# Second feed-forward of a two-layer diffusion backbone: more block steps between down tiles, x parked in DRAM, first queries ahead of later values

## The chip, the core and the metric

The kernel runs on one core of a Trainium2 chip. Its engines are PE (TensorE, matrix products; PEld is its weight load), DVE (VectorE), ACT (ScalarE) and POOL (GpSimd); SP (SyncE) issues nearly all DMAs. The metric is the device time of one execution in microseconds, the median of several runs. Everything is float32; each product of two float32 matrices is made from rounded high parts and remainders, as three matmuls.

## The reference

Two layers work on 512 tokens of width 1024 (`x`), with 256 context tokens.

```python
for i in range(DEPTH):                      # 2 layers
    h = modulate(rms_norm(x, norm_g[i, 0]), sh1, sc1)        # sh, sc, g: silu(c) @ mod_w[i] + mod_b[i]
    if i % 2 == 0:   # 4 global heads (qk-norm, rotary) and 4 windowed heads with a sink
        y, yc = attention_mixers(h, hc, ...)
    else:            # real part of a 2-D FFT over 4 channel groups, then a linear map
        y = fourier_mix(h) @ w_f
    x = x + g1 * rms_norm(y, norm_g[i, 1])
    h = modulate(rms_norm(x, norm_g[i, 2]), sh2, sc2)
    x = x + g2 * rms_norm(conv_ffn(h, ...), norm_g[i, 3])

def conv_ffn(h, w_up, conv_w, conv_b, w_down):
    u = h @ w_up                            # 1024 -> 2 x 2816
    u = depthwise width-3 convolution of u along the tokens, plus conv_b
    gate, val = jnp.split(u, 2, axis=-1)
    return (jax.nn.silu(gate) * val) @ w_down
```

## The kernel before

Data lie with channels on the 128 partitions: `xT`, `yT`, `hh` and `hl` are 128 x 8 x 512. The code is written as one long program; a scheduler then places each instruction on its engine's queue by its place in the text and by when its inputs and buffers are expected, and adds the semaphores. So the order in a queue can differ from the written one. `held`, `fence` and `follow` pin some of it.

**Splits.** `split(h, l, src)` (its two instructions have line L121) makes the high part on ACT and the remainder on DVE; `mm3` (L98, L99, L100) issues the three matmuls. Weights come by `raw` (L130, three buffers, loaded on SP's queue) and are split into `wpair` (five buffers for each part).

**The feed-forward** (`ffn`, run for layers 0 and 1). 2816 hidden channels are 22 blocks of 128, `fi` 0 to 21. An *up step* makes gate and value of one block. A plain step is 2 x 8 x 3 matmuls 512 columns wide. A *block step* (`seven_products`, for the `fi` in `SEVEN[l]`) splits the product in 2 x 2 blocks and needs seven block products instead of eight, 7 x 4 x 3 matmuls 256 wide; DVE adds weights for it (L1124 to L1127), ACT copies partial sums (L1158 to L1168) and DVE merges them (L1166, L1169). Its combined inputs are made once by `seven_inputs`, at `fi == SUMS[l]`, in place in `yT`. After either, `conv` (L1220 on ACT, L1221 and L1223 on DVE) and `gated` (L1233, L1234 and a split) leave the pair `gs[fi]` in `xp.pair` (four buffers of two blocks).

**Down tiles.** `GROUPS` cuts the 22 blocks in three groups of 8, 6 and 8. After the last up step of a group, eight tiles `d` of 128 output channels are made in a row: `weights(d)` loads and splits the down weights, `part(d, hs)` runs the matmuls (24 or 18 of 512 columns) and copies to `yT` (first group) or adds to it (L1341). The remaining `gemv` of layer 1 (L422, L425 on DVE; products of the conditioning vector) is pumped along with the tiles. The last group runs on halves of the tokens: first half of all tiles, then `mid` (norm sums, `boundary`, `x_update` at L297 and L299 and the output DMAs of the first half) while PE makes the second half, then the second half's tail.

In layer 0, `gemv_jobs` already stores `xT` to the DRAM tile `away`, uses its memory for weights, and loads it back (L407, L434).

**Attention's projections.** After the global keys and values come three groups of `w_in` columns, in the order `kb` (windowed keys, three blocks of tokens), `vb` (windowed values, three blocks) and `qa` (queries of heads 0 and 1, two blocks; `q_out` norms and rotates them into `Q`, which is `yT`'s memory). `keys(0)` (transposes of `K` on PE) and `values(0)` are placed beside the query blocks. Beside all of them `gate`, a `gemv_early`, makes two modulation vectors on DVE (L476, L478): each takes eight 0.5 MB loads into five places, three in `yT` and two in the context's buffer. Then `queries_t(0)` transposes the first head's queries (L949) and attention begins, with the other queries' projections as filler.

Of the kernel before, what the change touches and what calls it, by code (L numbers as in the profile page):

```python
# [10 lines left out]
F32 = mybir.dt.float32  # L11
# [18 lines left out]

GROUPS = [(0, 8), (8, 6), (14, 8)]

# [3 lines left out]

SEVEN = [(5, 6, 8, 10, 12, 14, 15, 17, 18, 20), (8, 9, 11, 12, 14, 15, 17, 18, 20)]
NSKEW = [6, 5]
# [37 lines left out]
def kernel(ctx: ExitStack, tc: tile.TileContext, a):  # L76
# [380 lines left out]
    def gemv_early(jobs, places, accs, pps):  # L457
        ws = {}

        def load(n):  # L460
            if n < KC * len(jobs):
                (l, v), k = jobs[n // KC], n % KC
                ws[n] = places[n % len(places)]()
                SY.dma_start(out=ws[n], in_=a["mod_r"][6 * l + v - 2, k // 2][:, k % 2, :])

        for n in range(3):
            load(n)
        yield
        for n in range(3, len(places)):
            load(n)  # L470
        yield
        ends = []
        for n in range(KC * len(jobs)):
            acc, k = accs[n // KC], n % KC
            if k == 0:
                V.tensor_scalar(out=acc, in0=ws[n], scalar1=scol[:, 0, k:k + 1], scalar2=None, op0=ALU.mult)  # L476
            else:
                V.scalar_tensor_tensor(out=acc, in0=ws[n], scalar=scol[:, 0, k:k + 1], in1=acc, op0=ALU.mult,  # L478
                                       op1=ALU.add)
            load(n + len(places))  # L480
            yield
            if k == KC - 1:
                ends.append(gemv_end(*jobs[n // KC], acc, pps))
            elif k in (1, 3):
                for e in ends:
                    next(e, None)
        yield
        for _ in range(2):
            next(ends[-1], None)
            yield  # L490
# [37 lines left out]
    with ExitStack() as es:  # L528
# [29 lines left out]
        with ExitStack() as e1:  # L558
# [281 lines left out]
            blocks = [(hh, hl, 0, 2), (hh, hl, 2, 4), (ch, cl, 0, 0)]  # L840
            for g, kind in enumerate(["kb", "vb", "qa"]):
                ws = group_weights(g)
                if g == 2:
                    v_kv = []
                if g == 2:
# [351 lines left out]

    def ffn(l, xp, ready, pre, mid, gem, plain=None):
        ys = YStat(late=xp.pool if l == 0 else None)
        skew = NSKEW[l]  # L1200
# [31 lines left out]
        def gated(fi, cg, cv, f0):  # L1232
            S.activation(out=cg, in_=cg, func=AF.Silu)  # L1233
            V.tensor_tensor(out=cv, in0=cg, in1=cv, op=ALU.mult)  # L1234
# [4 lines left out]
            gs[fi] = (gh, gl)  # L1239


# [23 lines left out]
        else:  # L1265
# [30 lines left out]
            sweep(range(skew), halves[1], range(SWEEP[1], KC))  # L1296
            remod(1, *n2, R[1], eng=V)
            first[skew] = first[skew][:3] + (mk(pps, [P, T], F32, "mm", 6),)
        if l == 0:
            pump(gem)  # L1300
        cg = None
        for u, (fi, i, w, ps) in enumerate(first):
# [13 lines left out]
            :, :, NF:], scalar1=-1.0, scalar2=None, op0=ALU.mult)  # L1316
        for gi, (f0, nch) in enumerate(GROUPS):
            end = gi == len(GROUPS) - 1
            for fi in range(max(f0, FIRST), f0 + nch):
# [11 lines left out]
                if l == 0 and fi not in SEVEN[l]:  # L1331
                    pump(gem, GP[0])
            g_ = [gs[fi] for fi in range(f0, f0 + nch)]
            ws = {}

            def part(d, hs, ps=None):
                ps, sl = y_mm(pps, ws[d], g_, hs, True, ps)
                if gi == 0:
                    S.copy(out=yT[:, d, sl], in_=ps[:, sl])
                else:  # L1340
                    V.tensor_tensor(out=yT[:, d, sl], in0=yT[:, d, sl], in1=ps[:, sl], op=ALU.add)  # L1341
                if end:
                    ys.add(pps, yT[:, d, sl], hs)

            def weights(d):
                r = raw([P, nch, P], a["w_down%d" % gi][l, d])
                wh, wl = (xp.spare if end and 4 <= d < 7 else wpair)([P, nch, P])
                split(wh, wl, r)
                ws[d] = [(wh[:, c, :], wl[:, c, :]) for c in range(nch)]

# [265 lines left out]
def _layout(i):  # L1616
# [29 lines left out]
    out = {}  # L1646
    for h, (f0, n) in enumerate(GROUPS):
        out["w_down%d" % h] = wd[:, f0:f0 + n].transpose(0, 3, 2, 1, 4)
    wf = i["fourier_w_out"][0].reshape(4, 256, D)
# [25 lines left out]
```

## Time and profile before

| what | us |
|---|---|
| median of 3 runs | 1147.99 (1147.73 to 1148.07) |
| the profiled execution | 1147.63, of which the span is 1145.9 |
| PE busy / DVE busy / ACT busy / POOL busy | 1115.4 / 872.4 / 577.6 / 176.6 |
| second feed-forward from its first full-width up step to the last matmul of its last group | 801.6 to 1132.6 |
| its last group of down tiles | 1085.9 to 1132.6 |
| windowed keys, values and first queries to the start of attention | 73.2 to 127 |

The profile is one execution. "Busy" is the time in which an engine worked on instructions; waits and DMA issues are not counted. Matmuls are pipelined and their shown ends overlap the next one, so the distance between starts tells how long one takes. In rows of the timeline the columns are start, length, engine, line, operation, tiles (out<-in), shape and count, and in brackets the idle time before it with what ended it. In rows by line, the numbers behind the first bar are busy us and mean ns of one, behind the second the engine's idle time before them. In rows by window, busy us and counts of PE, PEld, DVE, ACT and POOL follow the length, then the granted PE clock, the DMA share and GB/s. DMA rows give KB each and us from issue to landing.

### The profile page before, as it was taken

To read this page: it belongs to the slowest core of one execution; us is meant where nothing else is said; L and a number is where in the kernel's file an instruction comes from. 1 tells how busy PE (TensorE), PEld (TensorE's weight loads), DVE (VectorE), ACT (ScalarE), POOL (GpSimd) and SP (SyncE) were. 2 spreads that over 40 slices of the span, in tenths; PEclk is the share of its full clock that TensorE was granted. 3 is DMA by queue.
4 is the path that set the end of the run, shared out by engine and by line. 5 is a ranking of instruction groups with operands and counts; after the bars stand their busy time and mean duration, and the time that the engine had idled before them with its cause. 6 is when DMAs were issued, how large, how long until landed. Compare 5 with 4: busy or idle time off the path is not lost.

```text
span 1145.9 us, 19121 instructions
## 1 busy us (share of the span) xinstructions
PE 1115.4 (97%) x7658; PEld 962.8 (84%) x7658; DVE 872.4 (76%) x1418; ACT 577.6 (50%) x1030; POOL 176.6 (15%) x184
## 2 busy tenths in 40 slices
PE   8999999999999999999999999899999999999995
PEld 5689988868898978887898898879887888899895
DVE  4678777765679976987998668878997498679745
ACT  4342356666665633552465445557743355256442
POOL 1136332521420000000000143610000000000023
PEclk9999999999999999999999999999999999999998
DMA  9676101075142355535525301920227123223212
GB/s 366 248 239 215 43 1 38 8 263 208 38 184 111 117 194 207 218 122 209 187 108 183 122 2 37 291 88 28 74 95 270 58 92 111 101 84 111 93 56 74
DMA packets 31745, 151.61 MB, mean 132 GB/s; under 512 B 3236, under 2 KB 7972, under 8 KB 19752
## 3 DMA queue, kind: packets, MB, share of 16 engines
q1 hardware_dynamic: 30504, 146.19, 35.9%
q0 software_dynamic: 1152, 4.19, 1.5%
q8 instruction: 60, 0.98, 0.4%
q14 instruction: 29, 0.24, 0.1%
HBM read 146.18 MB, written 4.19 MB: 131 GB/s over the span
## 4 chain that ended last, share of the span: by engine, by line
PE 84%; DVE 7%; ACT 5%; DMA 2%; issue 1%; POOL 0%; DVEq 0%; SPq 0%; ACTq 0%; POOLq 0%
PE mm L98 24%; PE mm L99 23%; PE mm L100 23%; PE PT L920 1%; ACT wh L121 1%; PE O L98 1%; PE gm L498 1%; PE gm L98 1%; PE O L99 1%; PE gm L100 1%; PE gm L99 1%; PE mm L173 1%; PE O L100 1%; DVE md_t L230 1%; DMA xT<-in_mod_r 1%
## 5 line engine op out<-in xcount | busy, mean ns | idle before, releaser
L121 ACT CAST wh<-raw 128x1024 fp32r<-128x1024 f32 (+2 forms) x189 | 180.4, 966 | 188.8 <-PE mm L99 131.3
L121 DVE TENSOR_TENSOR wl<-raw,wh 128x1024 fp32r<-128x1024 f32 (+3 forms) x179 | 203.4, 1144 | 62.8 <-ACT wh L121 62.5
L98 PE MATMUL mm<-hh,wh 128*128 128x256 f32 (+2 forms) x652 | 220.8, 339 | 1.4 <-ACT yT L895 1.0
L99 PE MATMUL mm<-hl,wh 128*128 128x256 f32 (+2 forms) x652 | 218.4, 335 | 0.0
L100 PE MATMUL mm<-hh,wl 128*128 128x256 f32 (+2 forms) x652 | 218.1, 335 | 0.0
L272 POOL TENSOR_TENSOR gacc<-gacc,sq 128x256 f32<-128x256 f32 (+1 forms) x33 | 28.4, 862 | 714.2 <-ACT sq L270 713.5
L98 PEld LDWEIGHTS mm<-hh,wh 128*128 128x128 f32 x652 | 122.5, 188 | 18.9 <-ACT sq L1160 2.8
L99 PEld LDWEIGHTS mm<-hl,wh 128*128 128x128 f32 x652 | 122.6, 188 | 14.0
L100 PEld LDWEIGHTS mm<-hh,wl 128*128 128x128 f32 x652 | 122.6, 188 | 13.8
L98 PE MATMUL mm<-xh,wh 128*128 128x512 f32 (+1 forms) x368 | 132.0, 359 | 0.0
L99 PE MATMUL mm<-xl,wh 128*128 128x512 f32 (+1 forms) x368 | 130.8, 356 | 0.0
L100 PE MATMUL mm<-xh,wl 128*128 128x512 f32 (+1 forms) x368 | 130.3, 355 | 0.0
L98 PE MATMUL mm<-zh,wh 128*128 128x256 f32 x304 | 86.8, 286 | 0.0
L99 PE MATMUL mm<-zl,wh 128*128 128x256 f32 x304 | 84.6, 278 | 0.0
L100 PE MATMUL mm<-zh,wl 128*128 128x256 f32 x304 | 84.3, 277 | 0.0
L98 PEld LDWEIGHTS mm<-xh,wh 128*128 128x128 f32 x368 | 69.3, 188 | 12.8 <-issue 2.1
L99 PEld LDWEIGHTS mm<-xl,wh 128*128 128x128 f32 x368 | 69.2, 188 | 11.1 <-issue 0.4
L100 PEld LDWEIGHTS mm<-xh,wl 128*128 128x128 f32 x368 | 69.2, 188 | 10.8
L1220 ACT ACTIVATE cv<-mm,cols 128x512 f32<-128x512 f32 x64 | 49.6, 776 | 26.5 <-PE mm L100 23.5
L98 PEld LDWEIGHTS mm<-zh,wh 128*128 128x128 f32 x304 | 57.2, 188 | 3.5 <-ACT sq L1163 2.7
L100 PEld LDWEIGHTS mm<-zh,wl 128*128 128x128 f32 x304 | 57.2, 188 | 0.0
L99 PEld LDWEIGHTS mm<-zl,wh 128*128 128x128 f32 x304 | 57.1, 188 | 0.0
(423 smaller groups left out, 2669.3 us busy)
## 6 DMA issues: line engine op xcount, KB each, us to landing
raw<-in_w_up SPq DMA_DIRECT2D x42, 1024.0 KB, 4.9
xT<-in_mod_r SPq DMA_DIRECT2D x20, 1024.0 KB, 4.9
raw<-in_w_down SPq DMA_DIRECT2D x32, 512.0 KB, 4.2
raw<-in_mod_p SPq DMA_DIRECT2D x8, 1024.0 KB, 5.0
raw<-in_w_in SPq DMA_DIRECT2D x6, 1024.0 KB, 7.9
raw<-in_w_down SPq DMA_DIRECT2D x16, 384.0 KB, 3.1
yT<-in_mod_r SPq DMA_DIRECT2D x10, 512.0 KB, 5.9
raw<-in_w_out SPq DMA_DIRECT2D x4, 1024.0 KB, 4.9
```

Of the source, the lines that this page charges most:

```text
L98: i = PE.matmul(out, lhsT=ah, rhs=bh, start=start, stop=False, skip_group_check=skip)
L99: PE.matmul(out, lhsT=ah, rhs=bl, start=False, stop=False, skip_group_check=skip)
L100: return i, PE.matmul(out, lhsT=al, rhs=bh, start=False, stop=stop, skip_group_check=skip)
L121: i = S.copy(out=h, in_=src), eng.tensor_tensor(out=l, in0=src, in1=f(h), op=ALU.subtract)
L173: PE.matmul(ps[:32, :src.shape[1]], lhsT=ones32, rhs=src, start=True, stop=True)
L230: V.scalar_tensor_tensor(out=t, in0=src, scalar=am, in1=R, op0=ALU.mult, op1=ALU.mult)
L272: G.tensor_tensor(out=self.acc[:, sl], in0=self.acc[:, sl], in1=sq[:, sl], op=ALU.add)
L498: PE.matmul(ps[32 * q:32 * q + 32, :], lhsT=spad[:, k, :], rhs=w[:, q * T:(q + 1) * T], start=k == 0, stop=k == KC - 1)
L920: PE.transpose(out=pt[:, j * P:(j + 1) * P], in_=Ps[j][:, off:off + P], identity=ident)
L1220: S.activation(out=cv, in_=ps, func=AF.Identity, bias=bc, scale=wc[1])
```

## The change

1. Layer 1's groups become 4, 6, 6 and 6 blocks, and block steps are made for all `fi` from 8 to 21 (14 instead of 9).
2. The down tiles of a group that isn't the last are no longer made in a row at its end: `down_tiles` is a generator that the next group's steps pump, as many tiles after step `fi` as `DOWN[fi]` says. `gemv` rides on the tiles of the second and third group.
3. With groups overlapping, more pairs are alive. After the modulation in layer 1 `xT` is stored to `away`, and its memory holds the pairs of `fi` 0 to 3 and later of 10 to 13; before the last group's tiles `xT` is loaded back.
4. In attention's projections the order becomes `kb`, `qa`, `vb`; `keys(0)` and `values(0)` follow the first value block; `gemv_early` loads its second vector into the two context places alone, since the queries now take `yT` earlier.
5. The down weights are laid out as one array for each layer and group.

```diff
-GROUPS = [(0, 8), (8, 6), (14, 8)]
+GROUPS = [[(0, 8), (8, 6), (14, 8)], [(0, 4), (4, 6), (10, 6), (16, 6)]]
...
-SEVEN = [(5, 6, 8, 10, 12, 14, 15, 17, 18, 20), (8, 9, 11, 12, 14, 15, 17, 18, 20)]
+SEVEN = [(5, 6, 8, 10, 12, 14, 15, 17, 18, 20), (8, 9, 10, 11, 12, 13, 14, 15, 16, 17, 18, 19, 20, 21)]
+
+DOWN = {8: 4, 9: 4, 10: 1, 11: 1, 12: 1, 13: 2, 14: 1, 15: 2, 16: 1, 17: 1, 18: 1, 19: 2, 20: 1, 21: 2}
...
         def load(n):
             if n < KC * len(jobs):
                 (l, v), k = jobs[n // KC], n % KC
-                ws[n] = places[n % len(places)]()
+                ws[n] = places[n % len(places) if n < KC else 3 + n % 2]()
...
-            load(n + len(places))
+            if n + len(places) < KC:
+                load(n + len(places))
+            for m in {3: (8,), 4: (9,)}.get(n, (n + 2,) if n >= KC else ()):
+                load(m)
...
-            for g, kind in enumerate(["kb", "vb", "qa"]):
+            for g, kind in ((0, "kb"), (2, "qa"), (1, "vb")):
...
-                        pump(gate, 2 if kind == "vb" else 1)
+                        pump(gate, 2 if kind == "qa" else 1)
...
-                        if t0 == 0:
-                            keys(0, [(mk(pps, [P, T], F32, "misc", 2), n) for n in (2, 4)])
-                        else:
-                            v_kv.append(values(0))
                         q_out(0, t0, ps)
+                    if kind == "vb" and kb == 2:
+                        keys(0, [(mk(pps, [P, T], F32, "misc", 2), n) for n in (2, 4)])
+                        v_kv.append(values(0))
...
-                gs["t"] = xp.pair([P, 2, T])
+                gs["t"] = places.pop(0) if l and (f0 == 0 or f0 == 10 and fi < 14) else xp.pair([P, 2, T])
...
+        def down_part(gi, w, g_, d, hs, ps=None, end=False):      # the former part(d, hs)
+        def down_weights(gi, nch, d, pairs):                      # the former weights(d)
+        def down_tiles(gi, nch, g_):
+            yield
+            for d in range(KC):
+                down_part(gi, down_weights(gi, nch, d, wpair), g_, d, [0, 1])
+                if gi:
+                    pump(gem, GP[1])
+                yield
...
             remod(1, *n2, R[1], eng=V)
+            SY.dma_start(out=away, in_=xT)
+            xp2 = mk(cp, [P, 2, 2, 2, T], F32R, "xT")
+            places = [(xp2[:, i, 0], xp2[:, i, 1]) for i in (0, 1, 0, 1)]
...
-        for gi, (f0, nch) in enumerate(GROUPS):
+        down = iter(())
+        for gi, (f0, nch) in enumerate(GROUPS[l]):
...
+                if l:
+                    pump(down, DOWN.get(fi, 0))
+            pump(down, 100)
+            if l and end:
+                xT = mk(cp, [P, KC, T], F32, "xT")
+                SY.dma_start(out=xT, in_=away)
             g_ = [gs[fi] for fi in range(f0, f0 + nch)]
+            if l and not end:
+                down = down_tiles(gi, nch, g_)
+                pump(down)
+                continue
```

More of the change, by code (lines that the diff above doesn't have):

```diff
@@ L844 @@
                     v_kv = []
-                if g == 2:
+                if g == 1:
                     w_q = group_weights(3)
@@ L1198, in ffn @@
     def ffn(l, xp, ready, pre, mid, gem, plain=None):
+        nonlocal xT
         ys = YStat(late=xp.pool if l == 0 else None)
@@ L1239, in gated @@
             gs[fi] = (gh, gl)
+        def down_part(gi, w, g_, d, hs, ps=None, end=False):
+            ps, sl = y_mm(pps, w, g_, hs, True, ps)
+            if gi == 0:
+                S.copy(out=yT[:, d, sl], in_=ps[:, sl])
+            else:
+                V.tensor_tensor(out=yT[:, d, sl], in0=yT[:, d, sl], in1=ps[:, sl], op=ALU.add)
+            if end:
+                ys.add(pps, yT[:, d, sl], hs)
+        def down_weights(gi, nch, d, pairs):
+            r = raw([P, nch, P], a["w_down%d%d" % (l, gi)][d])
+            wh, wl = pairs([P, nch, P])
+            split(wh, wl, r)
+            return [(wh[:, c, :], wl[:, c, :]) for c in range(nch)]
+        def down_tiles(gi, nch, g_):
[5 more added lines that the diff above has]
+                yield
         first = []
@@ L1316, in ffn @@
             :, :, NF:], scalar1=-1.0, scalar2=None, op0=ALU.mult)
-        for gi, (f0, nch) in enumerate(GROUPS):
-            end = gi == len(GROUPS) - 1
+        down = iter(())
+        for gi, (f0, nch) in enumerate(GROUPS[l]):
+            end = gi == len(GROUPS[l]) - 1
             for fi in range(max(f0, FIRST), f0 + nch):
@@ L1332, in ffn @@
                     pump(gem, GP[0])
+                if l:
[4 more added lines that the diff above has]
+                SY.dma_start(out=xT, in_=away)
             g_ = [gs[fi] for fi in range(f0, f0 + nch)]
+            if l and not end:
+                down = down_tiles(gi, nch, g_)
+                pump(down)
+                continue
             ws = {}
             def part(d, hs, ps=None):
[L1337 to L1343, printed above, removed]
+                down_part(gi, ws[d], g_, d, hs, ps, end)
             def weights(d):
[L1346 to L1349, printed above, removed]
+                ws[d] = down_weights(gi, nch, d, xp.spare if end and 4 <= d < 7 else wpair)
             hs = {d: [0, 1] if not end or d == 0 else [0] for d in range(KC)}
@@ L1646, in _layout @@
     out = {}
-    for h, (f0, n) in enumerate(GROUPS):
-        out["w_down%d" % h] = wd[:, f0:f0 + n].transpose(0, 3, 2, 1, 4)
+    for l, groups in enumerate(GROUPS):
+        for g, (f0, n) in enumerate(groups):
+            out["w_down%d%d" % (l, g)] = wd[l, f0:f0 + n].transpose(2, 1, 0, 3)
     wf = i["fourier_w_out"][0].reshape(4, 256, D)
```

## The prediction

> **What bounds the kernel now.** I read the head of the profile first, then the chain of waits, then busy time by stage of the second feed-forward block (801 to 1146 us).
>
> ```profile
> span 1145.9 us, 19121 instructions
> PE 1115.4 (97%) x7658; PEld 962.8 (84%) x7658; DVE 872.4 (76%) x1418; ACT 577.6 (50%) x1030; POOL 176.6 (15%) x184
> PE 84%; DVE 7%; ACT 5%; DMA 2%; issue 1%; POOL 0%; DVEq 0%; SPq 0%; ACTq 0%; POOLq 0%
> ```
>
> PE is busy for 97% and carries 84% of the chain, so a matmul taken away is worth its time unless another engine then ends the wait. The stages below (columns: stretch, length, then busy us and instructions of PE, PEld, DVE, ACT, POOL) say which engine could.
>
> ```profile
> 801.60:858.40 56.80, 56.80 (x244) 45.73 (x245) 54.02 (x82) 34.45 (x46) 0.00 (x0) 1.00 0.23 78
> 967.20:1000.80 33.60, 33.60 (x145) 27.08 (x145) 20.39 (x25) 8.33 (x10) 0.00 (x0) 1.00 0.24 78
> 1021.60:1032.80 11.20, 11.20 (x51) 9.01 (x50) 10.97 (x16) 6.41 (x10) 0.00 (x0) 1.00 0.04 15
> 1032.80:1053.40 20.60, 20.54 (x170) 19.86 (x169) 18.32 (x24) 13.10 (x21) 0.00 (x0) 1.00 0.44 147
> 1032.70:1064.50 31.80, 31.74 (x218) 28.87 (x217) 29.29 (x39) 19.52 (x31) 0.00 (x0) 1.00 0.32 105
> 1085.90:1132.60 46.70, 46.69 (x380) 44.88 (x380) 22.98 (x41) 18.22 (x32) 13.03 (x16) 1.00 0.17 57
> ```
>
> Row three is one plain up step (fi 16), row four two block steps in a row (17 and 18); the timeline of PE gives their edges by the change of width.
>
> ```profile
> 1021.58 0.40 PE L98 MATMUL mm<-hh,wh 128*128 128x512 f32 x1
> 1032.78 0.28 PE L98 MATMUL mm<-hh,wh 128*128 128x256 f32 x1
> 1053.38 0.40 PE L98 MATMUL mm<-hh,wh 128*128 128x512 f32 x1
> ```
>
> PE is full in all of these. DVE is close behind where block steps stand (29.29 of 31.80 us over two block steps and a plain one) and in the opening (54.02 of 56.80), and idles in down tiles (20.39 of 33.60). So the second feed-forward is PE-bound with DVE as the next limit.
>
> **Part 1, five more block steps.** A plain step is 2x8x3 = 48 matmuls of 512 columns, a block step 7x4x3 = 84 of 256. By the edges, plain takes 1032.78 - 1021.58 = 11.20 us, block (1053.38 - 1032.78)/2 = 10.30 us. Steps 10, 13, 16, 19 and 21 change over: 5 x 0.90 = **-4.5 us** on PE. The Trainium skill ("TensorE: Matmul & The Clock Gate", "Wait — 56ns, not 53.3ns?") puts warm matmuls N/2.4 GHz + 2.5 ns apart, by which 48 wide ones would be 10.4 us, 84 narrow ones 9.2 us and this term an estimated -5.9 us. The trace does not agree: 11.20/48 = 233 ns and 10.30/84 = 123 ns against the page's 216 and 109, and the measurement decides.
>
> The price is on DVE. Its rows for the second feed-forward (mean ns ahead of the last bar):
>
> ```profile
> L121 DVE TENSOR_TENSOR wl<-raw,wh 128x1024 fp32r<-128x1024 f32 x59 | 71.9, 1222 | 26.8 <-ACT wh L121 26.7
> L1124 DVE TENSOR_TENSOR raw<-raw 128x1024 f32<-128x1024 f32 x9 | 11.0, 1220 | 0.2
> L1126 DVE TENSOR_TENSOR raw<-raw,raw 128x512 f32<-128x512 f32 x9 | 6.2, 685 | 0.1
> L1166 DVE TENSOR_TENSOR mm<-mm,sq 128x512 f32<-128x512 f32 x9 | 6.2, 694 | 0.7 <-PE mm L100 0.7
> L1221 DVE SCALAR_TENSOR_TENSOR cv<-mm,cols,cv 128x511 f32<-128x511 f32 x30 | 22.3, 745 | 6.3 <-ACT cv L1220 5.9
> L1234 DVE TENSOR_TENSOR cv<-cv,cv 128x512 f32<-128x512 f32 x22 | 15.1, 686 | 0.4
> L121 DVE TENSOR_TENSOR wl<-raw,wh 128x768 fp32r<-128x768 f32 x8 | 7.6, 953 | 3.2 <-ACT wh L121 3.2
> L1341 DVE TENSOR_TENSOR yT<-yT,mm 128x512 f32<-128x512 f32 x9 | 6.2, 684 | 11.2 <-PE mm L100 11.2
> L425 DVE SCALAR_TENSOR_TENSOR gacc<-raw,scol,gacc 128x1024 f32<-128x1024 f32 x7 | 9.0, 1283 | 1.8 <-DMA raw<-in_mod_r 1.7
> ```
>
> A block step: weight sums 1.22 + 2x0.69, splits 3x1.22 + 0.69, merges 2x0.69, convolution 4x0.745, gating 2x0.69: 12.7 us. A plain step: 2x1.22 + 2.98 + 1.37 = 6.8. Two and one make 32.2 against the 29.29 busy in their window (the rows' ends overlap), a factor of 0.91: **11.5 us of DVE a block step, above PE's 10.3**. Block steps alone would be DVE-bound; that is what part 2 must cover.
>
> **Part 2, down tiles between the steps.** A 512-wide matmul is 0.233 us, so a tile of six chunks (18) is 4.2 us of PE (33.60/8 agrees) and 0.91 x (0.95 + 0.68) = 1.5 us of DVE; a tile of four is 2.8 us and 0.6. The down products are the same in number under either grouping: PE neither gains nor loses. A fourth group adds eight yT passes: eight copies on ACT become the first group's as before, eight more adds of 0.68 lie on DVE inside the 1.5 counted.
> - Steps 8 and 9 with four small tiles each: PE 20.6 + 22.4 = 43.0, DVE 23 + 5: free.
> - Steps 10 to 12, one tile of six each: PE 14.5, DVE 11.5 + 1.5 = 13.0, but the remaining gemv goes with these tiles, two L425 (2.3): 15.3. DVE falls 0.8 x 3 = 2.4 us behind; step 13, with two tiles (PE 18.7, DVE 16.8), takes 1.9 back. A step's first product needs one of its four split pairs and each of seven products lasts 1.47 us, so some 3 us of lateness is hidden. If the overlap of 0.91 were not had, the lag is 3 x (16.9 - 14.5) = 7.2 us. Bounds 0 to 4; I take **+0.5**, nearer the measured 29.29-in-31.80 that ran without a PE stop.
> - Steps 14 to 21: 13.0 of 14.5, or 16.0 of 18.7 against 14.5 of DVE: free. ACT has 13.10 busy in 20.60, so its tile cast fits.
> - The first block step. Before, eight tiles of 45 us lay between step 7 and step 8; now step 8 follows at once. Its weights (0.91 x 6.9 = 6.3 us of DVE) move into the end of the window that is 54.02 of 56.80 full. The wl and gacc work that filled DVE there in their place (tile weights, L425) moves out, about as much. Bounds 0 to 3.5 (6.3 less the 2.8 idle; no gain, as PE idles nowhere there); I take **+0.5**.
> - Wait order: on wpair (five buffers) a step holds four and a tile one, so the next step's first pair takes what product 1 left, 1.5 us into the step. On raw (three), a step's two, a tile's and gemv's are four a cycle, each up to 4.9 us of load (row below) and about 5 of use: 40 of the 43 buffer-us a cycle of 14.5 us offers. This is tight only while gemv runs, and counted in the 0 to 4.
>
> **Part 3, x to DRAM and back.** Queue and landing rows:
>
> ```profile
> away<-xT SPq DMA_DIRECT2D x1, 2048.0 KB, 6.9
> xT<-away SPq DMA_DIRECT2D x1, 2048.0 KB, 7.7
> raw<-in_w_down SPq DMA_DIRECT2D x16, 384.0 KB, 3.1
> raw<-in_w_up SPq DMA_DIRECT2D x42, 1024.0 KB, 4.9
> 99.16 0.33 SPq L130 DMA_DIRECT2D raw<-in_w_in  x1
> 100.43 0.33 SPq L464 DMA_DIRECT2D yT<-in_mod_r  x1
> 803.41 12.90 SPq L130 DMA_DIRECT2D raw<-in_w_up  x2
> 1118.37 0.42 DVE L299 TENSOR_TENSOR xT<-xT,md_t 128x256 f32<-128x256 f32 x1
> 1127.02 0.42 DVE L1341 TENSOR_TENSOR yT<-yT,mm 128x256 f32<-128x256 f32 x1 [2.41 <-PE mm L100]
> ```
>
> The store reads xT once it is final, and lands in 6.9 us; its first customer is the gated pair of fi 0. If it is issued before the weight load at 803.41 on SP it costs nothing; behind it, the cast of fi 0 holds ACT for a few us while weights of steps 4 and 5 are ready: 0 to 1, I take 0. The reload waits for the last matmuls that read the places (the last tile of group three) and so starts 1.4 us (six matmuls) before the end group. x itself is wanted first at L299, now 1118.37 - 1085.90 = 32 us into the end group and some 26 with six chunks: hidden. What is queued behind it on SP is not: the down weights of the last group, one 0.4 MB load per 2.1 us of PE. With three raw buffers, the loads of d 0 to 2 can go ahead of it: SP's order is not the written one (at 99.16 the last query weights, written deep inside the attention loop, were issued before gemv_early's load at 100.43, written earlier). d 3 then lands with the 2 MB ahead of it, about 8.6 us after the reload is issued, plus 1.8 us for cast and split, against a need 1.4 + 4.2 + 2x2.1 = 9.8 us after: 0.6 late. Bounds 0 (no wait) to 3 (d 4 late as well); I take **+1.0**.
>
> The last group with six chunks shortens the second-half stage by 7x6 = 42 narrow matmuls, 5 us, of work that stands earlier instead: the same sum. DVE, behind through the boundary, waits for PE again at 1127.02, 5.6 us ahead of the stage's end, so this uses up the cover and costs 0 to 0.5: I take 0.
>
> **Part 4, queries before later values.** PE and POOL around the start of attention:
>
> ```profile
> 127.05 0.44 PE L949 MATMUL PT<-con,yT 128*128 128x128 f32 x2 [1.63 <-DVE yT L771]
> PE S L100 <- DVE ql L121: 1.2, 1, 1.2
> 94.68 0.74 DVE L476 TENSOR_SCALAR sqx<-cT,scol 128x1024 f32<-128x1024 f32 x1
> cT<-in_mod_r SPq DMA_DIRECT2D x6, 512.0 KB, 5.1
> 99.31 13.21 POOL L802 TENSOR_SCALAR K<-K,krs 128x128 f32<-128x128 f32 x12 [4.58 <-DVE krs L159]
> 90.30:131.00 40.70, 39.06 (x329) 37.59 (x328) 31.60 (x57) 11.04 (x17) 19.27 (x17) 1.00 0.44 147
> ```
>
> PE stands 1.63 us at 127.05 until the second query block is rotated on DVE, its last projection having just ended. With three value blocks (17 us) behind the queries this is covered: **-1.6**. What is late next is the same for head 1, 1.2 us: I leave it. Against it: keys(0) now follows the first value block, about 108 us, and reads K which POOL finishes scaling at 99.31 + 13.21 = 112.5. If the transposes stand there in PE's order, PE waits up to 4.4 us; other value blocks can go first. Bounds 0 to 4.4, I take **+0.5**. gemv_early's second job begins at 94.68 (L476) and, with two places instead of five, needs three more rounds of load (5.1) and add (1.3), ending near 95 + 1.3 + 3 x 6.4 = 116, when the last value block runs; only its closing matmul is on PE, 0 to 2, I take 0. DVE has 9 us idle in the 40.70, enough to turn the query work 20 us earlier.
>
> **Sum**, from the profiled execution's 1147.63 (span 1145.9 plus 1.7 around it; the runs' median 1147.99 is 0.36 above): -4.5 - 1.6 + 0.5 + 0.5 + 1.0 + 0.5 = -3.6 us. On the median: **1144.4 us**.
>
> **Rivals.**
> - *Clean.* No new stop, and head 1's 1.2 us goes as well: -4.5 - 1.6 - 1.2 = 1140.7. For it: PE hardly stopped in pairs of block steps. Against: DVE margins of 10%.
> - *DVE becomes the limit in steps 10 to 12.* The full lag of 7.2 less 3 hidden, 4.2 in place of 0.5: 1148.1, no change. For it: 15.3 against 14.5 by the row sums. It decides once weights come more than 3 us late.
> - *Keys wait for POOL.* 4.4 instead of 0.5: 1148.3, no change.
> - *The reload blocks the down weights (the other side).* If SP holds the loads of d 0 to 2 behind the reload too, PE has 1.4 us of work and needs 8.6 + 1.8 = 10.4: a stop of 9.0 in place of 1.0, 1152.4. It decides where the first load of the last group is issued after the reload. The landing row of a load issued 0.73 us behind the earlier 2 MB reload shows the mechanism:
>
> ```profile
> DMA to landing us min/median/max: 9.4/9.4/9.4
> ```
>
> That is a 1 MB weight load (L130, at 605.8); its usual time is 4.9, so it stood behind the 2 MB. The Trainium skill ("DMA: Bandwidth & Descriptors", "Two DMAs through the same engine are not ordered") says that descriptors of one queue start in order; the 9.4 agrees, and the rule speaks for this rival. Against it: the inversion at 99.16.
>
> **How the numbers follow.** Forecast 0.47 (own range 1142 to 1146), clean 0.16, DVE 0.14, keys 0.09, reload 0.14. The runs shown spread by 0.03%; about 0.2% (2.3 us) is what a measurement of this kernel can tell from no change. Faster (below 1145.7): 0.43 of the forecast's and the clean case, and a little of DVE and keys where they come in part: 0.62. No change: the rest of these, 0.20. Slower: the reload, and DVE or keys together with a late d 3: 0.18. The range for 8 in 10 runs from the clean case, with 1 us of unpriced room, to the no-change cases with 1.9 above: 1139.7 to 1150.2; it leaves out most of the reload case.
>
> **What would show it.** Part 1: 14 L1124 rows on DVE in the second feed-forward, each block step near 10.3 us on PE. Part 2: tiles of 4.2 us between them; PE idle ahead of L98 released by ACT or DVE splits in 10 to 13 would be the DVE rival. Part 3: SP's order around xT<-away, and PE's idle time at the last group. Part 4: no wait on yT before PT L949; a wait on POOL K before the first PE K transpose would be the keys rival. The prediction is wrong if block steps between tiles take 11 us or if PE stops more than 4 us in all at these places.

## The result, and the profile after

The changed kernel takes 1162.36 us (median of 4 runs, 1157.66 to 1164.38) against 1148.03 for the kernel before beside it (1147.73 to 1148.86): a ratio of 1.0116, 95% interval 1.0098 to 1.0133. It is slower by 1.2%; the forecast was 1144.4, with 1150.2 as the upper end. The profiled execution is the fastest of the four: the others are 4.2 to 6.7 us longer at a mean granted clock of 0.988 to 0.990 instead of 0.993, and 0.3 to 0.5% of 1160 us, an estimated 3.5 to 5.8 us, is about that difference.

The head of the page and its chain, after the change:

```profile
span 1155.9 us, 19508 instructions
PE 1114.4 (96%) x7796; PEld 967.2 (84%) x7796; DVE 903.1 (78%) x1469; ACT 593.6 (51%) x1068; POOL 173.0 (15%) x184
PE 77%; DVE 12%; ACT 5%; DMA 3%; issue 2%; POOL 1%; DVEq 0%; SPq 0%; ACTq 0%; POOLq 0%
```

The span is 10.0 us longer while PE's busy time is 1.0 us less. DVE's share of the chain rises from 7 to 12%: PE now waits. Where, the stages of the second feed-forward block say (same columns as in the prediction): opening, steps 8 and 9 with the small tiles, steps 10 to 15, steps 16 to 21, last group; then two steps of the third stretch by themselves.

```profile
800.90:857.10 56.20, 56.17 (x242) 45.45 (x243) 54.10 (x83) 34.21 (x46) 0.00 (x0) 1.00 0.18 62
857.10:900.50 43.40, 42.82 (x264) 37.79 (x263) 34.38 (x46) 26.69 (x43) 0.00 (x0) 1.00 0.31 102
900.50:1007.30 106.80, 98.79 (x659) 88.41 (x659) 87.42 (x112) 51.62 (x82) 0.00 (x0) 0.98 0.35 128
1007.30:1105.40 98.10, 95.60 (x643) 86.01 (x642) 79.77 (x104) 52.44 (x82) 0.00 (x0) 1.00 0.31 103
1105.40:1142.70 37.30, 36.94 (x295) 35.02 (x294) 20.60 (x39) 13.25 (x28) 12.00 (x16) 1.00 0.32 117
915.10:929.20 14.10, 14.10 (x103) 13.12 (x102) 12.03 (x15) 6.65 (x13) 0.00 (x0) 1.00 0.50 178
929.20:949.50 20.30, 16.73 (x103) 14.92 (x102) 16.96 (x22) 9.40 (x15) 0.00 (x0) 0.92 0.34 123
```

By the prediction's steps, steps 10 to 15 hold six block steps and eight tiles, 6 x 10.3 + 8 x 4.2 = 95.4 us, and so do steps 16 to 21. They take 106.8 and 98.1: **11.4 and 2.7 us too long**. The small tiles went as forecast (43.4 against 43.0). Step 11 with its tile took 14.10, as forecast (14.5); step 12 with its tile took 20.30. In these 106.8 us DVE is busy for 87.42 only, and still PE waits for it. The longest of PE's waits from 900 to 1105 us and the longest of DVE's (total, times, longest single one):

```profile
PE mm L102 <- DVE wl L123: 7.2, 3, 3.3
```

```profile
DVE raw L1128 <- DMA raw<-in_w_up: 14.2, 7, 3.0
DVE gacc L427 <- DMA raw<-in_mod_r: 7.8, 3, 3.0
DVE mm L1170 <- PE mm L102: 5.2, 8, 1.3
DVE wl L123 <- ACT wh L123: 4.9, 4, 1.3
DVE gacc L424 <- DMA raw<-in_mod_r: 1.9, 1, 1.9
```

PE waits for split weights (`wl`), and DVE, which makes them, stood 23.9 us behind loads into `raw`: 14.2 for weights of the up steps, and 9.7 for the four loads of the gemv. The 9.7 all lie in steps 10 to 13; of the 14.2, 11.0 come later, in steps 16 to 21, where PE loses little. The queue of SP around steps 11 and 12, and then some rows of DVE, show the circle:

```profile
917.85 0.33 SPq L132 DMA_DIRECT2D raw<-in_mod_r  x1
919.59 0.33 SPq L132 DMA_DIRECT2D raw<-in_w_up  x1
926.29 0.33 SPq L132 DMA_DIRECT2D raw<-in_w_down  x1
936.54 0.33 SPq L132 DMA_DIRECT2D raw<-in_mod_r  x1
937.68 0.33 SPq L132 DMA_DIRECT2D raw<-in_w_up  x1
```

```profile
923.02 1.28 DVE L427 SCALAR_TENSOR_TENSOR gacc<-raw,scol,gacc 128x1024 f32<-128x1024 f32 x1 [1.99 <-DMA raw<-in_mod_r]
924.99 1.27 DVE L427 SCALAR_TENSOR_TENSOR gacc<-raw,scol,gacc 128x1024 f32<-128x1024 f32 x1
927.45 1.21 DVE L1128 TENSOR_TENSOR raw<-raw 128x1024 f32<-128x1024 f32 x1
932.36 0.68 DVE L1131 TENSOR_TENSOR raw<-raw,raw 128x512 f32<-128x512 f32 x1
934.17 4.35 DVE L123 TENSOR_TENSOR wl<-raw,wh 128x1024 fp32r<-128x1024 f32 x4
941.49 2.61 DVE L427 SCALAR_TENSOR_TENSOR gacc<-raw,scol,gacc 128x1024 f32<-128x1024 f32 x2 [2.98 <-DMA raw<-in_mod_r]
```

The gemv's load is issued at 917.85, when a buffer comes free; DVE comes to its product, waits 1.99 us for it, and only then begins the sums (L1128) and splits of step 12, 1.8 us before PE begins that step at 929.2; these free the buffers for the next load, at 936.54, which DVE again waits for. So the load (917.85 to 923.02, 5.2 us) and DVE's work behind it (923.02 to 936.54, 13.5 us without a stop) follow each other and make a round of 18.7 us. From one up load to the next there are 937.68 - 919.59 = 18.1 us, against 14.5 that PE needs.

### The profile page after: what moved, and what is told of

It is laid out like the page before. It is cut to its first block, busy times and chain, and to the rows that moved or that the text cites. A ratio compares the mean times of both kernels' runs of the same rounds, so it can differ in the third digit from the quotient of the medians.

```text
span 1155.9 us, 19508 instructions
## 1 busy us (share of the span) xinstructions
PE 1114.4 (96%) x7796; PEld 967.2 (84%) x7796; DVE 903.1 (78%) x1469; ACT 593.6 (51%) x1068; POOL 173.0 (15%) x184
## 4 chain that ended last, share of the span: by engine, by line
PE 77%; DVE 12%; ACT 5%; DMA 3%; issue 2%; POOL 1%; DVEq 0%; SPq 0%; ACTq 0%; POOLq 0%
PE mm L100 22%; PE mm L102 20%; PE mm L101 20%; PE PT L924 1%; DMA cT<-in_mod_r 1%; DVE wl L123 1%; DVE md_t L299 1%; PE gm L100 1%; ACT wh L123 1%; PE gm L102 1%; PE gm L101 1%; PE O L100 1%; PE gm L503 1%; PE O L101 1%; DVE md_t L232 1%
## 5 line engine op out<-in xcount | busy, mean ns | idle before, releaser
L123 DVE TENSOR_TENSOR wl<-raw,wh 128x1024 fp32r<-128x1024 f32 (+2 forms) x197 | 213.7, 1100 | 44.4 <-ACT wh L123 42.9
L102 PE MATMUL mm<-hh,wl 128*128 128x256 f32 (+1 forms) x632 | 203.9, 323 | 7.2 <-DVE wl L123 7.2
L100 PE MATMUL mm<-hh,wh 128*128 128x256 f32 (+1 forms) x632 | 206.7, 327 | 2.4 <-ACT sq L1164 1.1
L101 PE MATMUL mm<-hl,wh 128*128 128x256 f32 (+1 forms) x632 | 203.7, 322 | 0.0
L100 PEld LDWEIGHTS mm<-hh,wh 128*128 128x128 f32 x632 | 118.9, 188 | 18.7 <-ACT sq L1164 5.4
L100 PE MATMUL mm<-zh,wh 128*128 128x256 f32 x384 | 109.9, 286 | 2.0 <-ACT sq L1162 1.3
L100 PE MATMUL mm<-xh,wh 128*128 128x512 f32 (+1 forms) x302 | 107.5, 356 | 0.0
L101 PE MATMUL mm<-zl,wh 128*128 128x256 f32 x384 | 107.4, 280 | 0.0
L102 PE MATMUL mm<-zh,wl 128*128 128x256 f32 x384 | 107.3, 281 | 0.0
L101 PE MATMUL mm<-xl,wh 128*128 128x512 f32 (+1 forms) x302 | 106.9, 354 | 0.0
L102 PE MATMUL mm<-xh,wl 128*128 128x512 f32 (+1 forms) x302 | 106.3, 352 | 0.0
```

The source lines that it names most:

```text
L100: i = PE.matmul(out, lhsT=ah, rhs=bh, start=start, stop=False, skip_group_check=skip)
L101: PE.matmul(out, lhsT=ah, rhs=bl, start=False, stop=False, skip_group_check=skip)
L102: return i, PE.matmul(out, lhsT=al, rhs=bh, start=False, stop=stop, skip_group_check=skip)
L123: i = S.copy(out=h, in_=src), eng.tensor_tensor(out=l, in0=src, in1=f(h), op=ALU.subtract)
```

## The experiments

All ratios are to the kernel before, run beside each. "FFN length" runs, in the profiled execution, from the first 512-wide product on `hh` in the second feed-forward block to the start of its last down product; it is 330.8 us before and 341.7 after. "K stop" is PE's idle time ahead of the last K transposes, at 108 to 113 us. The last column has the stops of 0.8 us or more in the second feed-forward block and around the K transposes; the wait of 1.63 us at about 127 us in the kernel before is in every kernel without the attention part, too.

| kernel | ratio [95%] | median us | FFN length | stops of PE |
|---|---|---|---|---|
| changed kernel | 1.0116 [1.0098, 1.0133] | 1162.36 | 341.7 | steps 12 to 14, and K 2.81 |
| e_ffn_only | 1.0121 [1.0106, 1.0136] | 1160.68 | 341.9 | steps 12 to 14 |
| e_attn_only | 1.0030 [1.0021, 1.0039] | 1150.11 | 330.7 | K 2.63 |
| e_blocks_only | 1.0085 [1.0068, 1.0101] | 1157.16 | 340.5 | five, up to 1.99 |
| e_tiles_only | 1.0043 [1.0026, 1.0059] | 1150.75 | 332.0 | K 4.2 |
| e_gemv_no_load | 1.0026 [1.0015, 1.0038] | 1149.72 | 328.4 | K 4.84 |
| e_gemv_first_tiles | 1.0080 [1.0065, 1.0095] | 1156.16 | 335.4 | steps 8 and 9, up to 1.43, and K 4.2 |
| e_raw_free_early | 1.0067 [1.0052, 1.0083] | 1154.24 | 333.7 | step 13, 1.92, and K 4.2 |
| e_own_buffer | 1.0001 [0.9991, 1.0012] | 1146.87 | 329.5 | none |
| e_own_and_order | 0.9993 [0.9984, 1.0002] | 1146.65 | 329.8 | none |
| e_own_with_attn | 1.0024 [1.0012, 1.0036] | 1149.87 | 330.2 | K 3.0 |
| e_keys_mm | 1.0118 [1.0101, 1.0135] | 1159.81 | 343.2 | steps 12 to 14, 2.1 at 118 |
| e_gate_no_load | 1.0009 [1.0000, 1.0018] | 1148.47 | 331.0 | K 1.25, 0.92 at 119 |

**The two halves of the change.** First the changed kernel with the attention part as before (`gemv_early` with five places, values before queries):

> The changed kernel with attention's projections as before (kb, vb, qa, gemv_early with five places). The profile of the changed kernel gains 0.7 us ahead of the second feed-forward (the 1.63 us wait at 127 is gone, a new one of 2.8 us stands ahead of the K transposes). So about 0.7 us slower than the changed kernel in the profile, and 1158 to 1163; if the attention part hurt, it would be faster by more than 1 us.

Then the kernel before with the attention part alone:

> The kernel before with the attention part of the change alone. From the profile: -0.7 us, 1147.3. If the new wait of 2.8 us ahead of the K transposes can vary, between -1.6 and +1.2.

The feed-forward half alone is as slow as the changed kernel (1.0121 against 1.0116). The attention half, which by the prediction was to bring 1.1 us and by my expectation to cost 1.2 at most, costs 0.30% or 3.4 us by its runs, although its profiled execution shows the wait at 127 us gone. One profile says little here: in those of the seven other kernels below that keep this part with its loads and in the changed kernel's own, the second feed-forward block begins anywhere from 800.9 to 807.0 us (801.6 before), and the K stop (e_keys_mm has none) lasts from 2.6 to 4.8 us.

**Steps without tiles, tiles without steps.** The kernel before with fourteen block steps:

```
-SEVEN = [..., (8, 9, 11, 12, 14, 15, 17, 18, 20)]
+SEVEN = [..., (8, 9, 10, 11, 12, 13, 14, 15, 16, 17, 18, 19, 20, 21)]
```

> The kernel before with block steps at all of 8 to 21 and nothing else: groups of 8, 6 and 8, down tiles in a row. A block step needs two raw buffers of three there and nothing else is loaded beside it. Theory R: the raw ring is not the limit, so stops come only from DVE being at 11.5 against 10.3 us in runs of six and eight block steps: -4.5 us of matmuls, less than 6 us of stops, 1144 to 1150. Theory D: 1.2 us a step short, less 3 us hidden in each run: -4.5 + 4 + 7 = +6 us, 1153 to 1156.

and the changed kernel with the nine old ones:

```
-SEVEN = [..., (8, 9, 10, 11, 12, 13, 14, 15, 16, 17, 18, 19, 20, 21)]
+SEVEN = [..., (8, 9, 11, 12, 14, 15, 17, 18, 20)]
```

> The changed kernel with the nine block steps of before (8, 9, 11, 12, 14, 15, 17, 18, 20); groups, interleaving, x in DRAM and the attention order as changed. PE's matmuls are those of before. Theory R: a plain step has a raw buffer of its own instead of two, so the ring is relieved in every third step and most of the stops of the changed kernel go, but gemv's loads still meet step 11 and 12: stops of 2 to 5 us, 1149 to 1153. Theory D: DVE has 6.2 us less work in each plain step, no stop at all: 1146 to 1148. If it is as slow as the changed kernel less 4.5, the interleaving is at fault and not the block steps.

Of fourteen block steps with nothing between them, six and then eight in a row:

```profile
903.00:966.00 63.00, 58.68 (x466) 55.78 (x466) 53.68 (x70) 38.41 (x64) 0.00 (x0) 1.00 0.22 78
1005.00:1085.00 80.00, 74.14 (x580) 70.50 (x579) 70.50 (x92) 47.16 (x78) 0.00 (x0) 0.98 0.24 85
```

DVE is busy for 85 and 88% of them, and from 915 to 966, once the first step is over, for 49.92 of 51 us. From 900 to 1105 us PE waits 5.8 us for DVE's splits and 4.2 for ACT's copies of partial sums. The two rows of steps last 67.2 and 91.1 us by PE's timeline, 158.3/14 = 11.3 us a step, where the prediction had reckoned 11.5 us of DVE. So block steps do need tiles beside them, and 1157.16 us is more than either of my ranges. With nine of them the interleaving leaves no stop in the block at all, although the gemv's products stand at the same time there (904 to 955 us): its 1.0043 is the attention part's 1.0030 and 1.2 us of FFN length. Fourteen steps without tiles stop for want of DVE; why fourteen with tiles stop is the question of the next trials.

**The loads of the gemv.** The changed kernel, with the second feed-forward's gemv reading a part of `hh` that lies in SBUF instead of loading its matrix (the last modulation vector is then another):

```
                 if not places:
-                    load()
+                    ws.append(...)     # [P, 2, D] view of hh, no DMA
```

> The changed kernel, but the second feed-forward's gemv multiplies parts of hh, already in SBUF, instead of weights that it loads (its result is another; the DVE work is the same). Theory R (raw buffers): gemv's four loads are a fourth customer of three raw buffers, so a block step's weights are reloaded late and DVE stands in order behind the loads; without them the stops of 3.5, 2.9 and 1.3 us ahead of the block steps 11 to 13 go, steps 10 to 15 take about 98 us instead of 106.8, and the time falls to about 1149 to 1151. Theory D (DVE time: 15.3 us of work in a 14.5 us cycle): the work is all there, the stops stay within 2 us of what they are, 1156 to 1162.

The FFN length falls by 13.3 us, to 328.4, with DVE's products all there. The stretch of time that lost 11.4 us, now (the block begins 4.9 us later here), and DVE's last products of the gemv:

```profile
900.50:1007.30 106.80, 106.62 (x720) 95.97 (x719) 90.88 (x120) 58.90 (x91) 0.00 (x0) 1.00 0.30 102
```

```profile
889.81 2.60 DVE L427 SCALAR_TENSOR_TENSOR gacc<-hh,scol,gacc 128x1024 f32<-128x1024 f32 x2
```

PE is full, and DVE busier than in the changed kernel (90.88 against 87.42). But the scheduler has placed the products earlier: they run from 863.9 to 892.4 us, beside steps 8 and 9, where in the changed kernel they run from 904.2 to 964.0, beside steps 10 to 13. So this trial takes away the loads, and with them the gemv's DVE work in these steps. It does not tell the two apart; the next two trials do.

**Gemv at another place, and buffers freed sooner.** The gemv with the first group's tiles as well:

```
-                if gi:
-                    pump(gem, GP[1])
+                pump(gem, GP[1])
```

> The changed kernel, but gemv is pumped with the first group's tiles too, so that it runs beside steps 8 and 9, where DVE has 34 us of work in 43. Theory R: raw is free between the small tile loads there (2 MB instead of 4 MB), the stops of steps 11 to 13 go, a stop of up to 2 us may come at step 9: 1149 to 1153. Theory D: the same sign, since DVE has room there: 1150 to 1154. If the stops in steps 10 to 13 stay, neither is right.

and the splits of a block step in layer 1 in an order that frees its loaded buffer earlier:

```
-        ("1", a4[:, 0:1]), ("57", s[:, 0:2]), ("63", s[:, 2:4]), ("24", a4[:, 1::2])
+        ("1", a4[:, 0:1]), ("24", a4[:, 1::2]), ("57", s[:, 0:2]), ("63", s[:, 2:4])     # in layer 1 only
```

> The changed kernel, but in layer 1 the split pairs of a block step that read the loaded buffer (1 and 24) are made ahead of those that read the sums (57 and 63), so the loaded buffer is free two splits (some 2 to 4 us) earlier. Theory R: the next step's load starts that much earlier, the stops in steps 10 to 13 shrink by 2 to 3 us a step and the 1 us a step in 16 to 21 go: 1149 to 1154. Theory D: DVE's work is the same: within 2 us of the changed kernel.

The first moves the stops rather than removing them, and is slower than I expected: in its steps 8 and 9 stand

```profile
PE mm L102 <- DVE wl L123: 2.8, 3, 1.4
PE misc L441 <- DVE gacc L427: 1.4, 1, 1.4
```

```profile
884.69 2.60 DVE L427 SCALAR_TENSOR_TENSOR gacc<-raw,scol,gacc 128x1024 f32<-128x1024 f32 x2 [1.38 <-DMA raw<-in_mod_r]
```

Its products run from 869.6 to 887.3, ahead of step 10 and about where e_gemv_no_load has them, and its FFN length is 335.4 against 328.4. DVE's work is the same; what differs is that the gemv's loads go through the ring, and I put the 7.0 us down to that.

The second takes away 8.0 of the 10.9 us by which the FFN was longer. DVE's work is the same, and the gemv's products stay beside steps 10 to 13, from 907.8 to 960.4. The first of them, and DVE's waits for loads from 900 to 1105 us:

```profile
907.76 0.75 DVE L424 TENSOR_SCALAR gacc<-raw,scol 128x1024 f32<-128x1024 f32 x1 [0.19 <-DMA raw<-in_mod_r]
```

```profile
DVE raw L1128 <- DMA raw<-in_w_up: 3.0, 4, 1.4
DVE gacc L427 <- DMA raw<-in_mod_r: 0.5, 1, 0.5
```

They were 14.2 and 7.8. Two splits' time earlier for one load is enough to loosen the ring.

**A buffer of its own.** On e_ffn_only, the gemv's four loads go into a pair of activation buffers that is free in steps 4 to 13, the next load issued when the products of the last are done:

```
+    def gemv_own(l, v, xp, pps):
+        t = xp.pair([P, D])
+        def load(kk):
+            for i in range(2):
+                SY.dma_start(out=f(t[i]), in_=a["mod_r"][6 * l + v - 2, kk][:, i, :])
+        load(0)
+        yield
...                                     # two products, then load(kk + 1)
+            if l and gi == 1:
+                pump(gem)
-            ... gemv_jobs([(1, 5)], pps), plain)
+            ... gemv_own(1, 5, xp, pps), plain)
```

> The changed kernel with the attention part as before, and with the second FFN's gemv moved off the three raw buffers: its four loads go into one pair of activation buffers that is free in steps 10 to 13, each load issued as soon as the two DVE products of the one before it are done. Raw buffers theory: nothing of the gemv stands in the ring any more, so DVE no longer stops at the gemv's products and the PE stops of 3.5, 2.9 and 1.3 us in steps 11 to 13 go; what stays is the block step's own load behind its two buffers (about 1 us in a step, as in steps 16 to 21). FFN 1 from its first to its last product 331 to 334 us (341.9 without this edit), ratio about 1.003. Rival, DVE's own work is the limit in steps 10 to 13: the products are still there, 340 us and ratio 1.01.

With the other order of splits on top:

> The kernel of e_own_buffer, and besides in layer 1 the block step's weights are split in the order 1, 24, 57, 63, so that the loaded buffer comes free before the buffer of sums. Raw buffers theory: the load of the next step is issued two splits (about 2 us) earlier, the remaining stops of about 1 us a step go as well, and fourteen steps at about 10.3 us against nine give what the change was priced at: FFN 1 325 to 328 us, ratio 0.995 to 0.998, faster than both kernels. Rival, DVE's work or the order of the splits limits steps 10 to 21: 332 us or more, ratio 1.003 or more.

And with the attention part kept:

> The changed kernel whole, attention part too, with one edit: the second FFN's gemv has a buffer of its own, as in e_own_buffer. Theory, two separate costs that add: the gemv in the raw ring (gone here) and the attention part (+3.4 us by e_attn_only, still here). Then the 3 stops of 933 to 974 us are gone, FFN 1 is 329 to 331 us long, the stop at 110 us stays, and the ratio is 1.002 to 1.004. Rival, the two parts share a cause (the earlier start or the fallen clock of the attention part makes the FFN late): the ratio stays above 1.006 or FFN 1 is longer than 333 us.

Every load and product of the gemv is still done, and the stops are gone. Of e_own_buffer, the same stretch, some rows of SP's queue, all that PE waited for from 900 to 1105 us, and DVE's last product of the gemv:

```profile
900.50:1007.30 106.80, 106.28 (x729) 96.13 (x728) 90.21 (x118) 57.76 (x91) 0.00 (x0) 1.00 0.31 103
```

```profile
914.99 0.33 SPq L132 DMA_DIRECT2D raw<-in_w_up  x1
929.32 0.33 SPq L132 DMA_DIRECT2D raw<-in_w_up  x1
```

```profile
PE mm L100 <- ACT sq L1185: 0.3, 1, 0.3
```

```profile
894.30 1.27 DVE L408 SCALAR_TENSOR_TENSOR gacc<-xl,scol,gacc 128x1024 f32<-128x1024 f32 x1
```

The up loads are 14.3 us apart. The load of step 12 goes out at 914.99, 16.7 us ahead of that step's first product (931.7); in the changed kernel it went out at 919.59, 9.6 us ahead (929.2). From 1.0121 to 1.0001: the gemv's place in the ring beside steps 10 to 13 cost 13.8 us of 1147.7, or 12.4 by FFN length. That is its loads and its DVE work together, for the products run earlier here as well, from 859.7 to 895.6, before step 10 begins at 902.1. Of the loads alone, e_raw_free_early gives 8.0 us of FFN length, with the products in place, and e_gemv_first_tiles some 7.0 in the other place. How much of the remaining 4.2 us (333.7 in e_raw_free_early against 329.5) is DVE's work stays open: no trial left the products beside steps 10 to 13 with their loads outside the ring. The edit also issues each load further ahead; whether the other place or the earlier issue does it was not tried.

My expectation was too cautious here (1.003) and too hopeful on the order of splits: nothing was left for it to free (329.8 against 329.5, and 0.9993 with an interval that holds 1). Neither kernel is measurably faster than the one before.

With the attention part kept the ratio is 1.0024: the attention's 0.30% is still there, within its interval, and no third cost shows.

**The K transposes.** In the changed kernel PE stands still until 109.93, and among DVE's rows ahead of that are these:

```profile
109.93 0.63 PE L554 MATMUL misc<-con,K 128*128 128x128 f32 x4 [2.81 <-DVE mods L453]
```

```profile
100.68 1.39 DVE L480 SCALAR_TENSOR_TENSOR sqx<-cT,scol,sqx 128x1024 f32<-128x1024 f32 x1 [0.88 <-DMA cT<-in_mod_r]
104.74 1.28 DVE L480 SCALAR_TENSOR_TENSOR sqx<-cT,scol,sqx 128x1024 f32<-128x1024 f32 x1 [0.84 <-DMA cT<-in_mod_r]
106.67 1.37 DVE L480 SCALAR_TENSOR_TENSOR sqx<-cT,scol,sqx 128x1024 f32<-128x1024 f32 x1 [0.65 <-DMA cT<-in_mod_r]
107.97 1.74 DVE L123 TENSOR_TENSOR wl<-raw,wh 128x1024 fp32r<-128x1024 f32 x1
109.63 0.15 DVE L453 TENSOR_TENSOR mods<-misc,cols 128x8 f32<-128x8 f32 x1
```

The transposes need a PSUM buffer of the tag `misc` (two). One holds the first modulation vector until the small add L453 has read it, and that add stands in DVE's order behind products of the second vector, each waiting for its load in one of the two places. Two trials. In the changed kernel, the transposes into PSUM buffers of the tag `mm`:

```
-        keys(0, [(mk(pps, [P, T], F32, "misc", 2), n) for n in (2, 4)])
+        keys(0, [(mk(pps, [P, T], F32, "mm", 6), n) for n in (2, 4)])
```

> The changed kernel, but the transposes of keys(0) get two of the six projection buffers of PSUM instead of the two that gemv_early's closing products also use. In the changed kernel PE stood 2.8 us ahead of the last four transposes until DVE had read gemv's product out of such a buffer. If the buffer is the cause, that wait goes and the stretch up to the second feed-forward is 2 to 3 us shorter; if the cause is POOL's scaling of K, it stays (POOL had finished at 106.3, PE went on at 109.9).

And in e_attn_only, the second vector's eight loads left out:

```
-                SY.dma_start(out=ws[n], ...)
+                if n < KC:
+                    SY.dma_start(out=ws[n], ...)
```

> The kernel before with the attention part alone, and the loads of the early gemv's second vector left out (eight of sixteen; its products run on what the places hold, so the second modulation vector is wrong). Theory: the last K transposes wait 2.8 us at 110 us because DVE stands in order behind products that wait for these loads, in the two places left to them, and so comes late to the add that frees the PSUM buffer. Then the stop at 110 us goes or falls below 1 us, FFN 1 starts 2 to 3 us earlier than with the attention part alone (ratio 1.0030), ratio 0.999 to 1.001. Rival, DVE is late by its own work there (products, splits, K scaling): the stop stays at 2 us or more and the ratio at 1.002 to 1.003.

The other buffers take away the stop at 110, but no time (1.0118 against 1.0116): the next `misc` user stands instead, at 118 us:

```profile
PE misc L441 <- DVE qtm L159: 2.1, 1, 2.1
```

Without the loads, PE's longest waits between 90 and 131 us are

```profile
PE misc L553 <- DVE mods L451: 1.2, 1, 1.2
PE misc L439 <- DVE kl L121: 0.9, 1, 0.9
```

and the ratio falls from 1.0030 to 1.0009. The two intervals do not meet, so the loads are most of it. This rests on the runs: in the profiled execution a K stop of 1.25 us stays, where I had expected less than 1, and the second feed-forward block begins no earlier than in e_attn_only (802.5 us against 802.3), instead of 2 to 3 us earlier. The trial also takes 4 MB off the DMA queues, and what that alone does is not told apart. What is left of the stop I put down to DVE's own work in that stretch, which was not tested. That two places as such, and not the later start of the second vector, make the loads late was not tried either.

## Why the prediction was wrong, by its steps

**The step that failed is the gemv beside steps 10 to 13 in part 2: the wait order and DVE's lag, put together at +0.5 us in bounds of 0 to 4.** It cost 13.8 us by the runs, 12.4 by FFN length. The prediction named the ring: four buffers' worth of work for three buffers a cycle while the gemv runs, "40 of the 43 buffer-us a cycle of 14.5 us". Two things were wrong in that. A buffer was priced at load (4.9) plus use (5), 10 us; the up load issued at 919.59 held its buffer until 937.68, 18.1 us, for its splits stand in DVE's order behind the gemv's products, sums and gating. (The buffer of the sums, one of the four, has no load at all.) And a sum of holds does not see what waits for what: the gemv's load and DVE's work take turns, 5.2 and 13.5 us, so that from one such load to the next there are 18.5, 18.7 and 19.3 us (issues at 899.35, 917.85, 936.54 and 955.87). Three rounds at 14.5 instead would be 13.0 us less; the stretch lost 11.4. Steps 16 to 21, without the gemv, still take 98.1 us in the changed kernel and 96.0 in e_own_buffer (999.3 to 1095.3 by PE's timeline): lateness is carried on.

**The DVE rival named the place and the releaser** (PE ahead of products, released by `wl`, in steps 10 to 13; it was 12 to 14) and the right amount of DVE work, 15.3 us a round against 14.5: from 923.02 to 941.49 DVE works for 15.5 us and waits 2.98 for the load. Of the 4.0 us by which that round is too long, the work is 1.0 and the load 3.0; the load is what the rival lacked. e_gemv_no_load and e_own_buffer cannot refute it, for there the gemv's work has left these steps; e_raw_free_early, where it has not, shows the loads' part by itself.

**Part 1, -4.5: right in price, less in yield.** Block steps are 10.32 us before; in e_own_buffer the thirteen that no tile cuts average 10.44. Fourteen at 10.44 against nine at 10.32 and five plain ones of 11.20 are -2.7 us; the first block step's stops (0.7, 0.4 and twice 0.2 at 852 to 864 us by the distances between starts, against +0.5 taken) take more than half of that back. FFN length falls by 1.3, which the runs do not tell from nothing (1.0001). DVE as next limit, 11.5 us a block step, was right (11.3). The line on steps 14 to 21 gives a step with two tiles 16.0 us of DVE and then 14.5; 11.5 + 2 x 1.5 is 14.5, and the step is free either way.

**Part 3, +1.0: too dear.** The reload rival is refuted by SP's queue in the changed kernel: six down loads of the last group went out ahead of the reload.

```profile
1091.72 8.79 SPq L132 DMA_DIRECT2D raw<-in_w_down  x6
1105.64 0.33 SPq L1371 DMA_DIRECT2D xT<-away  x1
1108.66 1.20 SPq L132 DMA_DIRECT2D raw<-in_w_down  x2
```

PE is busy for 36.94 of the 37.30 us of the last group: the reload costs 0.4 us at most.

**Part 4, -1.6 + 0.5: the wait went, and a larger one came.** The keys rival had the right instruction and the wrong releaser: POOL was done with `K` at 106.3, and it was the `misc` buffer behind `gemv_early`, which the prediction had set at "0 to 2, I take 0" because only a closing matmul is on PE. What counted was not the matmul but the add that frees its buffer, in order behind loads. By the runs the part is +3.4 us instead of -1.1.

What stays open: ring and attention do not add up in the changed kernel (e_ffn_only 1.0121, the whole 1.0116, where 1.0151 would be the sum), while they do in e_own_with_attn. The clock, below, may hide it; that was not tried. Nor was the attention part's 3.4 us taken apart further: in e_attn_only the K stop is 2.63 us and the stop at 127 us that went is 1.63.

## What to carry to other kernels

Where a ring of buffers is shared by loads of two kinds, count a buffer's hold from the issue of its load to the last in-order instruction that reads it, not load plus use. Then look for a circle, in which a load waits for an engine's work and that work for the load: a round takes the sum of both (18.7 us here), however idle the engine looks. A filler put between steps (here a gemv of 2.6 us a round) cost nothing measurable only where its loads had storage of their own, were issued well ahead, and its products stood beside other steps. When an add is the last reader of a scarce PSUM buffer, look for what stands ahead of it on its engine.

## What the hardware showed

The price of a stop is more than its length. After the stop of 3.33 us in step 12, some products of the changed kernel:

```profile
933.70 0.39 PE L102 MATMUL mm<-hh,wl 128*128 128x256 f32 x1 [3.33 <-DVE wl L123]
936.89 0.41 PE L102 MATMUL mm<-zh,wl 128*128 128x256 f32 x1
937.10 0.41 PE L100 MATMUL mm<-zh,wh 128*128 128x256 f32 x1
938.13 0.28 PE L102 MATMUL mm<-zh,wl 128*128 128x256 f32 x1
938.25 0.28 PE L100 MATMUL mm<-zh,wh 128*128 128x256 f32 x1
```

Products start 0.12 us apart at first, from 934.63 to 937.95 0.21 us apart, then 0.12 again: 3.3 us at little over half speed, an estimated 1.4 us lost besides the 3.33. The Trainium skill ("TensorE: Matmul & The Clock Gate", "Part 1: The HAM clock gate (the "warmup" mystery)") says that an idle window of some 3.4 us brings the clock to half, in free-running windows, and as much busy time brings it back. The halving and the way back agree. The length of the stop is less sharp here: the K stop of 2.63 us in e_attn_only is followed by a granted clock of 0.83,

```profile
110.00:120.00 10.00, 9.97 (x72) 10.00 (x73) 8.82 (x24) 1.90 (x5) 0.95 (x1) 0.83 0.50 149
```

while a similar one of 2.81 us in the changed kernel's profiled execution left it at 1.00 (a clock of 0.83 over 10 us is half speed for 3.4 of them). Counted over the profiled executions of all the kernels here, from 20 us on and without the last 15 us, stops of 1.0 to 1.7 us are not followed by a lower clock; of the 24 from 1.9 to 3.1 us, 18 are; and all seven from 3.3 us on have one in or behind them. So the length of a stop of 2 to 3 us does not tell whether half speed follows. Where it does, an estimated 1.4 to 1.7 us come on top for each stretch of 3.4 us.
